# A hybrid trunk layer on one NeuronCore: retention heads moved ahead of the stick-breaking heads of their round

## The chip, the cores and the metric

The kernel runs on one core of a Trainium2 chip. The metric is device time in microseconds (us). The kernel before took a median of 1002.31 us in 3 runs (1002.0 to 1005.52). "About no change" below means within 0.5%.

## What is computed

One layer over 544 rows of 1024 channels (512 rows of a new stream, 32 of a running one). Cut to what matters here:

```python
h = rmsnorm(x, norm_mix_w)
rq, rk, rv, rg, sq, sk, sv, ga, gb = split(h @ w_in)          # nine times 1024 columns
rq, rk = rotary(rq), rotary(rk) / 16                          # 4 retention heads, 256 wide
sq, sk = rmsnorm(sq, q_norm_w), rmsnorm(sk, k_norm_w)         # 8 stick-breaking heads, 128 wide
o_ret = chunkwise_retention(rq, rk, rv)                       # also the new state of each head
z = sq @ sk.T / sqrt(128);  u = log_sigmoid(-z) below the diagonal
o_sb = exp(log_sigmoid(z) + reversed_exclusive_cumsum(u)) @ sv
mix = sigmoid(ga) * rmsnorm(o_ret) * silu(rg) + sigmoid(gb) * o_sb
x = x + mix @ w_out
y = x + square(relu(rmsnorm(x) @ w_up)) @ w_down
```

## The kernel before, in words

Rows lie along the free axis (544 columns, in two halves of 272); channels lie on the 128 partitions. Every float32 product is made of three TensorE products of rounded parts (hi by hi, lo by hi, hi by lo). One **gemm** (function `gemm`) makes 128 output channels: 2 halves x 8 k-tiles x 3 = 48 matmuls of 128x272. Its weight tile comes by DMA on SP's queue (`load_w`), ACT casts it to `whi`, DVE subtracts to `wlo`. There are two buffers of each, so the cast for the gemm after next can't begin before a gemm has ended, and has to be done, `wlo` too, when the one in between ends. Each half goes to one of three PSUM banks (`mm`), which its reader on ACT or DVE gives back.

The order: first seven gemms on rows that are not yet normed (`X`, the input times the norm's weight; their readers multiply by the inverse root mean square `u` afterwards), while DVE and ACT make the normed rows `H`. Then four **rounds**. Round c has two stick-breaking heads (2c, 2c+1) with key, query and value gemms each, then retention head c with two gemms each for key, query and value (in round 0 some of them are among the seven on `X`). Then the **merge**: for each of 8 tiles a gemm for `rg`, one for `ga`, one for `gb`, whose readers on ACT are Sigmoids. Then the output projection and the MLP.

What a head does after its gemms is a **chain**, a Python generator that `Flow` cuts into pieces and puts between the matmuls of later gemms. `Flow` keeps a planned clock of PE, ACT and DVE, counts of free buffers, and runs a chain's next piece when its plan says that the inputs are ready (`poll`, after each k-tile). PE's order is this written order; ACT's and DVE's orders come from a scheduler. The chains named below:

- `sb_chain` (stick-breaking head): scores z into three of five `at` banks; ACT Abs, Exp, Ln; DVE adds max(z, 0) and splits into `sh`, `sl`; PE sums along the keys with the triangular `tri_r` and `neg1_r`; ACT Exp; DVE splits; PE multiplies by the values.
- `qk_chain` (QK norm): sums of squares by `ones_r`, then `rstd` on ACT (Ln, Exp, Square) and DVE.
- `sample_chain` (the 32 rows of the running stream, four heads at once): Abs, Exp, Ln, a scan, Exp, transposes, values.
- `retention_chain`, `ret_sample_chain` (which makes `so` by ACT and DVE and transposes it on PE) and `state_chain` (which transposes decayed keys, casts them to `kt`, and multiplies `rvs` by `kt`).

After the merge's second tile `flow.drain()` runs what is left of the chains. In the kernel before, that is retention head 3.

Of the kernel before, what the change touches and what calls it, by code (L numbers as in the profile page):

```python
# [16 lines left out]
D = 1024  # L17
# [17 lines left out]
IDLE = {0: 5, 1: 3}  # L35

MLP_W = 80
OUT_ORDER = (0, 4, 1, 5, 2, 6, 3, 7)


# [191 lines left out]
def trunk(ctx: ExitStack, tc: tile.TileContext, a: dict, g32):  # L232
# [11 lines left out]
    def tmp():  # L244
        return tp.tile([P, NT], F32, tag="tmp", name="tmp")
# [60 lines left out]
    def gemm(x, read, **parts):  # L306

        flow.wait(**parts)
        w = loaded.pop(0)
        load_w()
        for h in range(2):
            flow.wait(mm=1)
            ps = acc_bank()
            for k in range(KD):
                if x is H:
                    flow.pe = max(flow.pe, flow.done[("h", k)])
                products(ps, w, x, k, h)  # L320
                flow.poll()
            read(h, slice(h * HT, (h + 1) * HT), ps)
            flow.give(mm=1)
# [118 lines left out]
    def sb_value_tiles():  # L442

        hi = qkp.tile([P, 4, P], F32R, tag="vt_hi", name="vt_hi", bufs=2)
        lo = qkp.tile([P, 4, P], F32R, tag="vt_lo", name="vt_lo", bufs=2)
        return hi, lo, qkp.tile([P, P], F32, tag="vt_3", name="vt_3", bufs=2)
# [20 lines left out]
    def rope_tiles(tag):  # L467
        return [qkp.tile([P, NT], F32, tag=f"{tag}{d}", name=f"{tag}{d}") for d in range(2)]

    def rope(x, y, phase, c, n):  # L470


        def first(h, s, p):
            V.tensor_tensor(y[0][:, s], p, phase[0][:, s], op=ALU.mult)
            V.tensor_tensor(y[1][:, s], p, phase[1][:, s], op=ALU.mult)

        def second(h, s, p):
            t1, t2 = t.get()
            V.tensor_tensor(t1[:, s], p, phase[1][:, s], op=ALU.mult)
            V.tensor_tensor(t2[:, s], p, phase[0][:, s], op=ALU.mult)  # L480

        gemm(x, first)
        t = Tmps(2)
        gemm(x, second)
        flow.start(rope_chain(y, *t.get(), c, n))
# [44 lines left out]
    with tc.tile_pool(name="xin", bufs=1, side="right") as xp:  # L530
        xs = []
        x_hi = xp.tile([P, KD, NT], F32R, tag="x_hi", name="x_hi")
        x_lo = xp.tile([P, KD, NT], F32R, tag="x_lo", name="x_lo")
        for k in range(KD):
            t = xp.tile([P, NT], F32, tag=f"x{k}", name=f"x{k}")
            nc.sync.dma_start(out=t, in_=a["x"][k])
            xs.append(t)
            w = wv[:, 0, k : k + 1]
            if k == 0:
                split_scaled(t, w, x_hi[:, k, :], x_lo[:, k, :])  # L540
            else:
                S.activation(x_hi[:, k, :], t, AF.Copy, scale=w)
                V.scalar_tensor_tensor(
                    x_lo[:, k, :], t, w, x_hi[:, k, :].bitcast(F32), op0=ALU.mult, op1=ALU.subtract
                )
            if k in (0, 3):
                load_w()
        load_w(xp)
        nc.vector.tensor_scalar(nw[:, 0, :], wv[:, 0, :], -1.0 / (2 * D), None, op0=ALU.mult)
        nc.vector.tensor_scalar(nw[:, 2, :], wv[:, 2, :], -1.0 / 512, None, op0=ALU.mult)  # L550
        nc.vector.tensor_scalar(nw[:, 3, 0:1], wv[:, 3, 0:1], -(128.0 ** -0.5) / 256, None, op0=ALU.mult)
        nc.vector.tensor_scalar(nw[:, 3, 1:2], wv[:, 3, 1:2], -1.0 / 256, None, op0=ALU.mult)
        nc.sync.dma_start(out=cst, in_=a["cst"])
        X = (x_hi, x_lo)
        u = []

        def first_norm():
            acc = tmp()
            for k in range(KD):
                add_square(acc, xs[k], k == 0)  # L560
            flow.t = 16500.0
            parts = sum_parts(acc)
            yield need(at=2)
            sums = partition_sums(parts)
            flow.t += 2250
            with tc.high_priority():
                u.append(rstd(sums, D))
            flow.give(at=2)
            flow.finish("u")
            scaled(pa, ra, u[0])  # L570
            scaled(pb, rb, u[0])
            flow.give(at=1, mm=3)
            flow.finish("ab")
            flow.start(value_chain(ra, vt0, 0, vs[:, 0, :], ("v", 0), a["o_v"][0]))
            flow.start(value_chain(rb, rv0, 0, rvs0, ("rv0", 0)))
            yield need()
            for k in range(KD):
                t = tmp()
                V.scalar_tensor_tensor(t, xs[k], nw[:, 0, k : k + 1], u[0], op0=ALU.mult, op1=ALU.mult)
                split(t, h_hi[:, k, :], h_lo[:, k, :])  # L580
                flow.finish("h", k)
                if k % 2:
                    yield need()
            flow.give(tmp=6)

        flow.wait(vt=2, rv=1, tmp=9, mm=3, at=1)
        vt0, vt1 = sb_value_tiles(), sb_value_tiles()
        rv0, rvs0 = ret_value_tiles()
        ra, rb, rc = tmp(), tmp(), tmp()
        pa, pb = (acc_bank(), acc_bank()), (acc_bank(), bank()[:, :HT])  # L590
        wa, wb = loaded.pop(0), loaded.pop(0)
        flow.start(first_norm())
        flow.pe = 6500.0
        for k in range(KD + 2):
            for ps, w, kk in ((pa, wa, k), (pb, wb, k - 2)):
                if 0 <= kk < KD:
                    for h in range(2):
                        products(ps[h], w, X, kk, h)
            for i in range(IDLE.get(k, 0)):
                nc.tensor.matmul(idle[:, :P], ones_r, ones_r, start=True, stop=True)  # L600
            flow.poll()
        flow.wait(at=2)
        pc = (bank()[:, :HT], bank()[:, :HT])
        w = loaded.pop(0)
        for k in range(KD):
            for h in range(2):
                products(pc[h], w, X, k, h)
            flow.poll()
            if k == 5:
                load_w()  # L610
        flow.until("ab")
        scaled(pc, rc, u[0])
        flow.give(at=2)
        flow.start(value_chain(rc, rv0, P, rvs0, ("rv1", 0)))
        flow.wait(tmp=1)
        rd = tmp()
        gemm(X, lambda h, c, p: V.scalar_tensor_tensor(
            rd[:, c], p, -1.0 / (2 * D), u[0][:, c], op0=ALU.mult, op1=ALU.mult
        ))
        flow.start(value_chain(rd, vt1, 0, vs[:, 1, :], ("v", 1), a["o_v"][1]))  # L620
        flow.wait(rk=1, tmp=2)
        rk0 = rope_tiles("rk")
        turned = [tmp(), tmp()]
        for t, c0 in zip(turned, (C_COS, C_SIN)):
            V.scalar_tensor_tensor(t, u[0], -1.0 / (2 * D), cst[:, c0 : c0 + NT], op0=ALU.mult, op1=ALU.mult)
        rope(X, rk0, turned, 0, 0)
        flow.give(tmp=2)
        query_key(0, 1, X, u[0])
        flow.until("h", KD - 1)

    bigp = at.enter_context(tc.tile_pool(name="bigp", bufs=1))
# [340 lines left out]
        leave(c)  # L972

    phase = (cst[:, C_COS:C_SIN], cst[:, C_SIN:C_TRI])
    for c in range(NH):
        for h in (2 * c, 2 * c + 1):
            for w_col in (1, 0):
                if (h, w_col) != (0, 1):
                    query_key(h, w_col)
            if c == 0:  # L980
                vt = (vt0, vt1)[h]
            else:
                flow.wait(vt=1)
                vt = sb_value_tiles()
                values(H, vt, 0, vs[:, h % 4, :], ("v", h), a["o_v"][h])
            flow.start(sb_chain(h, vt))
        if c % 2:
            flow.start(sample_chain(c // 2))
        x = []
        for n, tag in enumerate(("rk", "rq")):  # L990
            if c == 0 and n == 0:
                x.append(rk0)
                continue
            flow.wait(**{tag: 1})
            x.append(rope_tiles(tag))
            rope(H, x[n], phase, c, n)
        if c == 0:
            rv, rvs = rv0, rvs0
        else:
            flow.wait(rv=1)  # L1000
            rv, rvs = ret_value_tiles()
            for ei in range(2):
                values(H, rv, ei * P, rvs, (f"rv{ei}", c))
        sc = bigp.tile([P, 2, 256], F32, tag="sc", name="sc")
        nc.gpsimd.dma_start(out=sc, in_=a["state"][c].rearrange("(d p) e -> p d e", p=P))
        flow.start(retention_chain(c, rv))
        flow.start(ret_sample_chain(c, x[0], x[1], rvs, sc))
        flow.start(state_chain(c, x[0], rv, rvs, sc))


    mp = ctx.enter_context(ExitStack())
# [411 lines left out]
```

## Time and profile before

| | us |
|---|---|
| median of 3 runs | 1002.31 |
| the profiled execution | 1002.26 |
| its span | 1000.5 |
| PE busy | 986.7 |
| DVE busy | 668.0 |
| ACT busy | 522.7 |
| matmuls of 128x272 in a steady stream, from start to start | 0.125 |

PE's busy time is made of matmuls that overlap: each shows 0.29 us and they start each 0.125 us. A gap is therefore seen best from start to start; the number in brackets behind a row of the timeline counts from the modelled end of the matmul before. Times in the views are us from the span's start. The seven gemms on `X` end at 54.7 us, the four rounds at about 421 us, the merge begins there.

### The profile page before, as it was taken

The numbers are of one execution on the slowest core, as the hardware profiler recorded it, in microseconds if no ns is written. First come the engines' busy times: TensorE is split into PE (matmuls) and PEld (weight loads), VectorE is DVE, ScalarE is ACT, GpSimd is POOL, SyncE is SP. The second block draws the span as 40 slices with busy tenths as digits, with TensorE's granted clock in tenths as the row PEclk, the third lists the DMA queues.
The fourth block names the chain that finished last, engine by engine and source line by source line (L and its number), as shares of the span: only waits on it lengthen the run. The fifth ranks groups of instructions, "written<-read, shape, count | busy, mean of one in ns | idle before, by whom it ended". The sixth has DMA issues, their size and how long they took to land.

```text
span 1000.5 us, 18622 instructions
## 1 busy us (share of the span) xinstructions
PE 986.7 (99%) x7726; PEld 969.3 (97%) x7726; DVE 668.0 (67%) x1124; ACT 522.7 (52%) x963; POOL 47.2 (5%) x80
## 2 busy tenths in 40 slices
PE   9999999999999999999999999999999999999998
PEld 9999888999999999889999999999999999999998
DVE  7968768866677576756434447974676666676782
ACT  6466756537654675564333335775464445444440
POOL 0000003001000011000000011000000000000000
PEclk9999999999999999999999999999999999999999
DMA  7232224122322135114322245232223332343312
GB/s 253 87 128 75 86 75 149 64 85 96 108 64 85 64 125 164 45 51 165 97 87 85 85 142 185 85 127 85 85 93 101 103 106 87 104 129 96 119 43 90
DMA packets 30932, 102.71 MB, mean 103 GB/s; under 512 B 4096, under 2 KB 6144, under 8 KB 30848
## 3 DMA queue, kind: packets, MB, share of 16 engines
q1 hardware_dynamic: 24768, 80.88, 25.0%
q0 software_dynamic: 6080, 20.65, 6.2%
q8 instruction: 60, 0.98, 0.4%
q14 instruction: 24, 0.20, 0.1%
HBM read 90.51 MB, written 11.01 MB: 101 GB/s over the span
## 4 chain that ended last, share of the span: by engine, by line
PE 95%; ACT 2%; DVE 2%; issue 0%; ACTq 0%; DVEq 0%
PE mm L225 70%; PE at L225 25%; ACT tmp L225 1%; PE at L384 0%; DVE sl L225 0%; ACT e L225 0%; ACT whi L225 0%; ACT L225 0%; DVE tmp L225 0%; ACT kt L225 0%; DVE sh L225 0%; DVE e L225 0%; PE at L600 0%; DVE so L225 0%; ACT st L225 0%
## 5 line engine op out<-in xcount | busy, mean ns | idle before, releaser
L225 PE MATMUL mm<-h_hi,whi 128*128 128x272 f32 x1040 | 304.5, 293 | 0.0
L225 PE MATMUL mm<-h_hi,wlo 128*128 128x272 f32 x1040 | 301.1, 290 | 0.9 <-DVE wlo L225 0.9
L225 PE MATMUL mm<-h_lo,whi 128*128 128x272 f32 x1040 | 300.3, 289 | 0.0
L225 DVE TENSOR_TENSOR wlo<-raw,whi 128x1024 fp32r<-128x1024 f32 (+1 forms) x146 | 167.6, 1150 | 125.8 <-ACT whi L225 125.0
L225 ACT CAST whi<-raw 128x1024 fp32r<-128x1024 f32 (+1 forms) x146 | 144.8, 992 | 179.3 <-PE mm L225 162.1
L225 PEld LDWEIGHTS mm<-h_hi,whi 128*128 128x128 f32 x1040 | 196.7, 189 | 1.9 <-issue 1.3
L225 PEld LDWEIGHTS mm<-h_hi,wlo 128*128 128x128 f32 x1040 | 196.3, 189 | 1.1 <-DVE wlo L225 1.1
L225 PEld LDWEIGHTS mm<-h_lo,whi 128*128 128x128 f32 x1040 | 196.9, 189 | 0.1
L225 PE MATMUL mm<-u_hi,whi 128*128 128x272 f32 x512 | 147.9, 289 | 0.0
L225 PE MATMUL mm<-u_lo,whi 128*128 128x272 f32 x512 | 147.8, 289 | 0.0
L225 PE MATMUL mm<-u_hi,wlo 128*128 128x272 f32 x512 | 147.7, 288 | 0.0
L225 PEld LDWEIGHTS mm<-u_hi,whi 128*128 128x128 f32 x512 | 96.6, 189 | 0.4 <-DVE y L225 0.2
L225 PEld LDWEIGHTS mm<-u_lo,whi 128*128 128x128 f32 x512 | 96.5, 188 | 0.0
L225 PEld LDWEIGHTS mm<-u_hi,wlo 128*128 128x128 f32 x512 | 96.3, 188 | 0.0
L225 PE MATMUL at<-f_hi,wlo 128*128 128x272 f32 x320 | 92.7, 290 | 0.0
L225 PE MATMUL at<-f_lo,whi 128*128 128x272 f32 x320 | 92.2, 288 | 0.0
L225 PE MATMUL at<-f_hi,whi 128*128 128x272 f32 x320 | 92.1, 288 | 0.0
L225 ACT ACTIVATE tmp<-tmp 128x272 f32<-128x272 f32 (+2 forms) x148 | 75.4, 553 | 29.6 <-DVE tmp L225 29.1
L225 DVE TENSOR_TENSOR y<-mm,y 128x272 f32<-128x272 f32 x112 | 48.6, 436 | 29.3 <-PE mm L225 29.3
L225 PEld LDWEIGHTS at<-f_hi,whi 128*128 128x128 f32 x320 | 60.5, 189 | 0.0
L225 PEld LDWEIGHTS at<-f_lo,whi 128*128 128x128 f32 x320 | 60.4, 189 | 0.0
L225 PEld LDWEIGHTS at<-f_hi,wlo 128*128 128x128 f32 x320 | 60.3, 188 | 0.0
(234 smaller groups left out, 1795.0 us busy)
## 6 DMA issues: line engine op xcount, KB each, us to landing
raw<-in_w SPq DMA_DIRECT2D x142, 512.0 KB, 3.5
x<-in_x SPq DMA_DIRECT2D x8, 272.0 KB, 5.2
o_v<-tmp POOLq DMA_DIRECT2D x8, 272.0 KB, 2.4
o_k<-tmp POOLq DMA_DIRECT2D x8, 272.0 KB, 2.5
x<-in_x POOLq DMA_DIRECT2D x8, 272.0 KB, 3.6
o_y<-x POOLq DMA_DIRECT2D x8, 272.0 KB, 2.4
tmp<-o_y POOLq DMA_DIRECT2D x8, 272.0 KB, 3.8
o_y<-y SPq DMA_DIRECT2D x16, 136.0 KB, 1.7
```

The costliest lines, as they stand in the source:

```text
L225: f(out, *args, **kw)
```

## The change

The list `HEADS` now gives the order of the heads: R0 S0 S1 R1 S2 S3 R2 S4 S5 R3 S6 S7 (R is a retention head, S a stick-breaking one). So the retention head comes first in each round, and the last chains are those of stick-breaking heads 6 and 7. The seven gemms on `X` were sv0, rv0 (two), sv1, rk0 (two), sk0; they are now sv0, rv0 (two), rk0 (two), rq0 (two). The values of head 1 and the key of head 0 are made from `H`. The order of the weight tiles in memory follows.

```diff
+HEADS = "R0 S0 S1 R1 S2 S3 R2 S4 S5 R3 S6 S7".split()
...
-        flow.wait(vt=2, rv=1, tmp=9, mm=3, at=1)
-        vt0, vt1 = sb_value_tiles(), sb_value_tiles()
+        flow.wait(vt=1, rv=1, tmp=9, mm=3, at=1)
+        vt0 = sb_value_tiles()
...
-        flow.wait(tmp=1)
-        rd = tmp()
-        gemm(X, lambda h, c, p: V.scalar_tensor_tensor(
-            rd[:, c], p, -1.0 / (2 * D), u[0][:, c], op0=ALU.mult, op1=ALU.mult
-        ))
-        flow.start(value_chain(rd, vt1, 0, vs[:, 1, :], ("v", 1), a["o_v"][1]))
...
         rope(X, rk0, turned, 0, 0)
+        flow.wait(rq=1)
+        rq0 = rope_tiles("rq")
+        rope(X, rq0, turned, 0, 1)
         flow.give(tmp=2)
-        query_key(0, 1, X, u[0])
...
-    for c in range(NH):
-        for h in (2 * c, 2 * c + 1):
-            for w_col in (1, 0):
-                if (h, w_col) != (0, 1):
-                    query_key(h, w_col)
...
+    def stick_breaking(h):
+        for w_col in (1, 0):
+            query_key(h, w_col)
+        if h == 0:
+            vt = vt0
+        else:
+            flow.wait(vt=1)
+            vt = sb_value_tiles()
+            values(H, vt, 0, vs[:, h % 4, :], ("v", h), a["o_v"][h])
+        flow.start(sb_chain(h, vt))
+        if h % 4 == 3:
+            flow.start(sample_chain(h // 4))
+
+    def retention(c):
         if c == 0:
-            rv, rvs = rv0, rvs0
+            k, q, rv, rvs = rk0, rq0, rv0, rvs0
         else:
+            flow.wait(rk=1)
+            k = rope_tiles("rk")
+            rope(H, k, phase, c, 0)
+            flow.wait(rq=1)
+            q = rope_tiles("rq")
+            rope(H, q, phase, c, 1)
...
+    for kind, n in HEADS:
+        (stick_breaking if kind == "S" else retention)(int(n))
```

How it moves instructions. **ACT, at the merge's beginning.** `tmp<-mm` is a Sigmoid on a gemm's half, `e<-at` the Abs or the Exp of a stick-breaking head, `e<-e` its Exp or Ln, `whi<-raw` the cast of a weight tile, `kt` the decayed keys. Before:

```order
L225 ACTIVATE tmp<-mm 128x272
L225 CAST kt_5472<-at 128x512
L225 ACT_TABLE_LOAD
L225 ACTIVATE tmp<-at,epsb 128x512
L225 ACT_TABLE_LOAD
L225 ACTIVATE tmp<-tmp 128x512 x2
L225 COPY so_p<-at 128x512
L225 ACT_TABLE_LOAD
L225 ACTIVATE tmp<-mm 128x272
L225 CAST kt_5529<-at 32x256
```

Now, from the scores of head 7 on, in two pieces that follow each other (the second has head 7's casts `sh`, the Exp and Ln of the sample rows, `tmp<-tmp`, and head 7's last Exps):

```order
L227 ACTIVATE e<-at 128x512 x2
L227 ACTIVATE e<-at 128x256
L227 ACT_TABLE_LOAD
L227 ACTIVATE e<-e 128x1280
L227 ACT_TABLE_LOAD
L227 ACTIVATE tmp<-mm 128x272
L227 ACT_TABLE_LOAD
L227 ACTIVATE e<-e 128x1280
L227 CAST whi<-raw 128x1024
L227 ACT_TABLE_LOAD
L227 ACTIVATE tmp<-mm 128x272 x2
L227 CAST whi<-raw 128x1024
```

```order
L227 ACT_TABLE_LOAD
L227 ACTIVATE tmp<-tmp 128x544
L227 CAST sh<-e 128x128 x3
L227 ACT_TABLE_LOAD
L227 ACTIVATE tmp<-tmp 128x544
L227 ACT_TABLE_LOAD
L227 ACTIVATE e<-at 128x512
L227 ACT_TABLE_LOAD
L227 ACTIVATE tmp<-mm 128x272
L227 ACT_TABLE_LOAD
L227 ACTIVATE tmp<-tmp 128x544
L227 ACTIVATE e<-at 128x512
```

What moved: where four table loads stood in the whole merge before, sixteen stand now, one at each change between a Sigmoid and a chain's Exp or Ln, and one between Exp and Ln (the program has 19 loads in all, 7 before).

**ACT, in the sample rows of retention head 0** (`so` and `st` are theirs; `tmp<-at,epsb` and `tmp<-tmp` are Ln and Exp or Square of a QK norm). Before:

```order
L225 CAST qk_hi_1726<-tmp 128x512
L225 ACTIVATE so,st<-at 32x256
L225 ACTIVATE st<-st,epsb 32x1
L225 ACTIVATE st<-st 32x1 x2
L225 COPY tmp<-mm 128x272
```

Now:

```order
L227 ACTIVATE so,st<-at 32x256
L227 ACTIVATE tmp<-at,epsb 128x272
L227 ACTIVATE st<-st,epsb 32x1
L227 ACTIVATE tmp<-tmp 128x272
L227 ACTIVATE st<-st 32x1
L227 ACTIVATE tmp<-at,epsb 128x272
L227 ACTIVATE st<-st 32x1
L227 ACTIVATE tmp<-tmp 128x272 x3
```

What moved: the norm of head 0's key stands between the steps of `so`, which had ACT to themselves before.

## Rows read from the trace of the kernel before

**Rows 1.** The page: busy time, and the chain that ended last, by engine.

```profile
PE 986.7 (99%) x7726; PEld 969.3 (97%) x7726; DVE 668.0 (67%) x1124; ACT 522.7 (52%) x963; POOL 47.2 (5%) x80
PE 95%; ACT 2%; DVE 2%; issue 0%; ACTq 0%; DVEq 0%
```

**Rows 2.** Busy time by stretch (us; PE, PEld, DVE, ACT, POOL; granted clock; DMA share; GB/s).

```profile
26.00:54.00 28.00, 28.00 (x227) 27.95 (x227) 27.85 (x52) 13.43 (x28) 1.23 (x2) 1.00 0.24 78
85.00:165.00 80.00, 74.12 (x543) 69.67 (x542) 59.97 (x113) 52.76 (x119) 6.90 (x12) 1.00 0.27 88
```

**Rows 3.** PE's waits from 85 to 165 us: total, times, longest; three of eight.

```profile
PE at L225 <- DVE so L225: 1.3, 1, 1.3
PE at L225 <- DVE sl L225: 1.0, 1, 1.0
PE mm L225 <- DVE wlo L225: 0.9, 1, 0.9
```

**Rows 4.** Timeline of PE at the last chain's end (start, busy, row, [idle before <- releaser]).

```profile
449.01 0.29 PE L225 MATMUL mm<-h_hi,wlo 128*128 128x272 f32 x1
451.33 0.50 PE L225 MATMUL at<-rvs,kt 96*128 96x256 f32 x2 [2.03 <-ACT kt L225]
```

**Rows 5.** Busy time by stretch around that wait, columns as in rows 2.

```profile
448.84:452.26 3.42, 1.39 (x11) 1.17 (x10) 3.30 (x6) 2.80 (x6) 0.16 (x1) 1.00 0.22 77
452.26:455.67 3.41, 3.41 (x17) 3.41 (x16) 1.76 (x3) 0.00 (x0) 0.72 (x1) 0.50 0.79 265
455.67:459.08 3.41, 3.41 (x29) 3.41 (x28) 1.22 (x1) 1.47 (x3) 0.00 (x0) 1.00 0.74 275
```

**Rows 6.** Timeline of ACT before that wait.

```profile
446.23 1.30 ACT L225 ACTIVATE tmp<-tmp 128x512 f32<-128x512 f32 x2
...
448.02 1.28 ACT L225 ACT_TABLE_LOAD   x1
449.31 0.40 ACT L225 ACTIVATE tmp<-mm 128x272 f32<-128x272 f32 x1
449.60 0.35 ACT L225 CAST kt<-at 32x256 fp32r<-32x256 f32 x1
```

**Rows 7.** The way to so in retention head 0: timelines of ACT and DVE.

```profile
133.12 0.37 ACT L225 ACTIVATE so<-at 32x256 f32<-32x256 f32 x1
136.07 0.47 DVE L225 TENSOR_SCALAR so<-at,st 32x256 f32<-32x256 f32 x1
```

**Rows 8.** Timelines at the end of the gemms on X; the page's landing times on POOL's queue.

```profile
54.69 0.28 PE L225 MATMUL mm<-h_hi,whi 128*128 128x272 f32 x1
55.45 0.72 POOL L1005 DMA_DIRECT2D sc<-in_state  x1 [17.34 <-DVE neg_r L646]
x<-in_x POOLq DMA_DIRECT2D x8, 272.0 KB, 3.6
```

**Rows 9.** Timeline of ACT in sb_chain of head 0, and pieces of ACT at 406 us.

```profile
82.02 0.87 ACT L225 ACTIVATE e<-at 128x512 f32<-128x512 f32 x2 [0.16 <-PE at L225]
83.15 1.28 ACT L225 ACTIVATE e<-e 128x1280 f32<-128x1280 f32 x1
84.31 0.43 ACT L225 ACTIVATE tmp<-tmp 128x272 f32<-128x272 f32 x1
406.44 1.35 ACT L225 ACTIVATE tmp<-tmp 128x544 f32<-128x544 f32 x2
408.25 0.50 ACT L225 CAST sh<-e 128x128 fp32r<-128x128 f32 x2 [0.27 <-DVE e L225]
```

**Rows 10.** Timeline of DVE: the same head's e, a wlo, and the head's second split.

```profile
85.94 1.62 DVE L225 SCALAR_TENSOR_TENSOR e<-at,e 128x512 f32<-128x512 f32 x3 [1.90 <-ACT e L225]
89.13 1.22 DVE L225 TENSOR_TENSOR wlo<-raw,whi 128x1024 fp32r<-128x1024 f32 x1
105.86 0.83 DVE L225 CAST sh<-e 128x1280 fp32r<-128x1280 f32 x1
106.79 1.49 DVE L225 TENSOR_TENSOR sl<-e,sh 128x1280 fp32r<-128x1280 f32 x1
```

More of the change, by code (lines that the diff above doesn't have):

```diff
@@ L974, in trunk @@
     phase = (cst[:, C_COS:C_SIN], cst[:, C_SIN:C_TRI])
-    for c in range(NH):
-        for h in (2 * c, 2 * c + 1):
-            for w_col in (1, 0):
-                if (h, w_col) != (0, 1):
-                    query_key(h, w_col)
[L980 to L996, printed above, removed]
+    def stick_breaking(h):
[11 more added lines that the diff above has]
+    def retention(c):
         if c == 0:
-            rv, rvs = rv0, rvs0
+            k, q, rv, rvs = rk0, rq0, rv0, rvs0
         else:
+            flow.wait(rk=1)
[4 more added lines that the diff above has]
+            rope(H, q, phase, c, 1)
             flow.wait(rv=1)
@@ L1006, in trunk @@
         flow.start(retention_chain(c, rv))
-        flow.start(ret_sample_chain(c, x[0], x[1], rvs, sc))
-        flow.start(state_chain(c, x[0], rv, rvs, sc))
+        flow.start(ret_sample_chain(c, k, q, rvs, sc))
+        flow.start(state_chain(c, k, rv, rvs, sc))
+    for kind, n in HEADS:
+        (stick_breaking if kind == "S" else retention)(int(n))
     mp = ctx.enter_context(ExitStack())
@@ L1351 @@
     ws = []
-    ws += [sv[0], rv[0], rv[1], sv[1], rk[0], rk[1]]
-    for c in range(NH):
-        for h in (2 * c, 2 * c + 1):
-            ws += [sk[h], sq[h], sv[h]][: 2 if c == 0 else 3]
-        for p in (rk, rq, rv) if c else (rq,):
-            ws += [p[2 * c], p[2 * c + 1]]
+    ws += [sv[0], rv[0], rv[1], rk[0], rk[1], rq[0], rq[1]]
+    for kind, n in HEADS:
+        n = int(n)
+        if kind == "S":
+            ws += [sk[n], sq[n], sv[n]] if n else [sk[n], sq[n]]
+        elif n:
+            ws += [p[2 * n + i] for p in (rk, rq, rv) for i in range(2)]
     for t in range(KD):
```

## The prediction

> **What bounds the kernel now.** First the page's busy times and the chain that ended last [rows 1]: PE is busy 986.7 of 1000.5 us and holds 95% of the chain. Both programs give PE the same 7598 matmuls, so a new order can only win or lose PE's waits and the clock. Then the windows and PE's waits. In 85 to 165 us, where the first round's chains meet, PE is idle for 80.00 - 74.12 = 5.9 us [rows 2], in eight waits of which three stand in [rows 3]. Idle time counts from the modelled end of a matmul, 0.29 us after its start, where the stream would have gone on after 0.125; each wait costs some 0.15 us more, so about 7.0 us in all. The second place is the end of the last chain: PE's product of `rvs` and `kt` starts 451.33 - 449.01 = 2.3 us after the matmul before it [rows 4], which is 2.2 lost. Behind it the granted clock fell: after a stretch with 11 matmuls came one of 3.41 us at 0.50 (the 1.2 GHz level) with 17 records, where the next at full clock has 29 [rows 5]. 12 x 0.125 = 1.5 us lost. So the tail costs 2.2 + 1.5 = 3.7 us. What PE waited for there is ACT: its queue had table loads of 1.28 us each, one Sigmoid and then the cast `kt` [rows 6]. The rest of the rounds shows under 1.5 us of waits; they are built alike before and after, and I leave them at no change.
>
> **The change, part by part: the start.** Ahead of the first round, rq0 takes the place of sv1 and sk0 on `X`. DVE gets 8 reads of 272 columns, two sums and two splits in a stretch where it has no idle time (27.85 of 28.00 us) [rows 2]. It did 52 instructions there; from 27.0 us on it now has 51 of the same kinds (27.3 us by the same mean) up to the last normed rows, and waits for PE about 1 us: 55.5 us; PE begins with `H` at 54.7 [rows 8] and reaches the last k-tile 21 matmuls later, at 57.3. Covered, with 1.8 us to spare. POOL's loads for retention head 0 (`sc`, `dm`, `dec`) went out at 55.45 behind DVE's cast `neg_r` [rows 8]; that cast now stands behind the sums of rq0, at about 57.7. `dm` follows `sc` by 0.7 and lands 3.6 later, at 62.0; it is read when PE has done 57 gemm matmuls and six score products, at 63.3. Covered too, by 1.3 us. The next `dm` and `dec` now stand ahead of `o_k` of head 0 on POOL, but its key is finished later still. SP has the same weight tiles in another order.
>
> The old waits go: the second split of head 0 has 7 us of PE work before its values now, and the value copies of head 3 no longer stand between a chain and its banks. Two new ones come, both seen in the order of ACT.
> - `so` of retention head 0. From the last product PE to ACT takes 0.3. ACT now does 0.37 + 0.2 for `so` and, with the key's norm between, three pieces of 0.35 and three of 0.2 to 0.3: 2.3. DVE adds four short ones and a product of 544: 1.6. Together 4.2 us. PE has four sums and 12 matmuls, 2.0 us. Wait: **2.2** us. Before it took 136.07 - 133.12 us to the last step [rows 7], beside 18 matmuls. Bounds: 1.2 (that wait again) to 3.
> - `kt` of the sample rows. It is cast behind the norm of head 1's key: 0.25 to reach ACT, two Ln of 0.37, an Exp of 0.35, the cast 0.36, 1.7 us, while PE has three matmuls, 0.4. Wait: **1.3** us (0 to 2).
> - Two more are small differences of long sums (the sums of squares of sk1, the `wlo` of rk1's second tile), 0.45 each: **0.9** us (0 to 2).
>
> The start then keeps 4.5 of its 7.0 us: **-2.5** (from -5.8 to 0).
>
> **The tail.** The last chains are now those of heads 6 and 7 and of the sample rows; their Exp and Ln alternate with the merge's Sigmoids. Sixteen table loads stand there instead of four: 12 x 1.28 = 15.4 us more on ACT. What of it reaches PE I take from four places, with pieces from start to start: 1.29 a load, 0.3 a Sigmoid [rows 6], 0.3 the last Abs, 1.16 for 1280 columns, 0.6 for 544, 0.2 a cast `sh` [rows 9].
> - **Weights of ga1.** After head 7's last score: 0.25, Abs 0.3, load, Exp 1.16, load, Sigmoid 0.3, load, Ln 1.16 is 7.0; then DVE's three pieces of `e` 1.55 and `wlo` 1.2 [rows 10]: 9.7. The cast's buffer is free long before. PE has 6 + 48 + 2 matmuls, 7.0 us, until it needs `wlo`. Wait: **2.7**.
> - **Head 7's sums over keys.** After the sample scores: 0.25, Abs 0.35, load 1.29, Exp 0.6, two casts 0.4 is 2.9; PE has 6 matmuls and two products, 1.2. Wait: **1.6** (the table load and the Exp alone make it).
> - **The sample weights' transposes.** From there ACT does the third cast, load, Ln 0.6, load, Exp 0.5, load, Sigmoid 0.3, load, Exp 0.6: 7.4; PE has sums of 1.55 and 30 matmuls, 5.3. Wait: **1.9** (with the cast shared, 2.1 at most).
> - **Head 7's values.** Two Exps 0.8, then `sh` 0.83 and `sl` 1.49 [rows 10]: 3.0; PE has transposes, 9 matmuls and one product, 1.9. Wait: **1.1**.
>
> Sum 7.3 us. Bounds: 2.2 (no worse than now) to 11, if each place is 1 us later. The first hole, 2.7 us with two matmuls in it, is longer than the one behind which the clock fell before [rows 4, 5], so I count one fall, 1.5 us; bounds none to three. Tail 8.8 against 3.7: **+5.1** (from -1.5 to +11.8).
>
> On the loads a rule has to be weighed. In the trace the Sigmoid starts 449.31 - 448.02 = 1.29 us after the load's start, and the Exp before it follows a load as closely [rows 6]. The Trainium skill, "ScalarE: Activation LUTs", section "What ACT_TABLE_LOAD costs", gives about 1283 ns for the load and about 1380 ns for a drain with every switch, 2.66 us together. The load agrees with the row, the drain isn't seen in it. By the page twelve loads would add 31.9 us to ACT instead of 15.4.
>
> **Sum:** -2.5 + 5.1 = +2.6 us on the profiled execution's 1002.26: 1004.9. The median of the runs, 1002.31, is the same within 0.1 us.
>
> **The rivals.**
> - **The loads are covered.** If PE finds the chains done at the four places, the tail loses its 3.7 us and the start 2.5: 1002.3 - 6.2 = 996.1; with half of the waits left, about 999.5. For it: ACT is busy for 52% only [rows 1]. Against it: at the last chain a single queue of three loads already made 2.3 us [rows 4, 6]. It needs PE's 7.0 us at ga1 to outlast 9.7. Chance 0.10.
> - **The tail is ACT's, and the clock falls again** (slower). One fall stretches PE's next pieces, the sample scores come later, and all that ACT does behind them too. It decides as soon as the second hole also holds over 2 us: then two more falls, 3.0 us, and 1 us more at each of two places, 1002.3 + 2.6 + 5 = 1009.9. For it: the holes stand within 20 us. Against it: a fall that PE spends waiting anyway costs nothing. Chance 0.27.
> - **The start wins nothing.** DVE falls behind on rq0, PE waits at the first k-tiles of `H`, and the eight waits come back in other places: 1002.3 + 5.1 = 1007.4. For it: no idle time on DVE [rows 2]. Chance 0.12.
> - **The drain counts too.** With each switch some 1.4 us longer, the three, one and four loads at the first three places make 4.1, 1.4 and 5.5 us more, 1016. The rows show no such gap [rows 6]. Chance 0.01. This is the price of the skill's page named above.
> - The forecast: 0.50.
>
> **How the numbers follow.** A measurement of this kernel tells 0.5%, 5.0 us, from no change. Faster by more (under 997.3): most of the half-covered case stays inside, so 0.06. Slower by more (over 1007.3): most of the second rival (0.22), half of the third (0.06), the drain (0.01) and the forecast's upper bounds (0.05): 0.34. Within: 0.60. The range reaches from the half-covered case, 999.5, to 1010.5, just past the second rival.
>
> **What would show it.** Right: ACT with 19 table loads of 1.28 us; from 85 to 165 us PE idle for under 5 us, with a wait for `so` of about 2 us near 71 us; after the scores of head 7 a wait for `wlo` of over 2 us and three more of 1 to 2 us; the granted clock at 0.50 at least once there; the MLP unchanged. Wrong: no wait over 1 us in the merge (the loads are covered), or waits before 60 us (DVE is late). Were the sum of waits in the merge right and the time still near 1000, the start would have won more than I give it.

## The result and the profile after

The changed kernel took a median of 1008.81 us in 4 runs (1008.53 to 1009.9) where the kernel before took 1002.45 beside it: a ratio of 1.0059, 95% interval 1.0038 to 1.008. Run again later on another occasion (experiment e11) it took 1008.38 us, a ratio of 1.0044 (1.0031 to 1.0058). So it is slower, by about the 0.5% that the prediction set as its bound; 0.5% lies inside both intervals. The profiled execution took 1008.78 us, its span 1007.0.

The page of the changed kernel, busy times and the chain that ended last (against [rows 1]):

```profile
PE 989.6 (98%) x7726; PEld 969.5 (96%) x7726; DVE 665.6 (66%) x1120; ACT 539.4 (54%) x979; POOL 45.8 (5%) x80
PE 93%; ACT 4%; DVE 3%; issue 0%; DVEq 0%
```

ACT has 16 instructions and 16.7 us more, PE the same 7726 matmuls, DVE four instructions and 2.4 us less; ACT and DVE now hold 7% of the chain instead of 4%. The groups of ACT's table loads, first of the kernel before, then of the changed one (instructions, busy us, mean ns):

```profile
L225 ACT ACT_TABLE_LOAD x6 | 7.7, 1283 | 0.1
```

```profile
L227 ACT ACT_TABLE_LOAD x18 | 23.1, 1283 | 0.3
```

One more in each has a line of its own. Seven loads became 19; 12 x 1.283 = 15.4 us is nearly all of ACT's growth. Sixteen of them stand in the merge.

Where PE waits now, in the changed kernel from 55 to 180 us (total, times, longest; against [rows 3]), and then from 421 to 501 us, the merge up to its fourth tile:

```profile
PE at L227 <- DVE so L227: 2.0, 2, 1.9
PE at L227 <- ACT kt L227: 1.0, 1, 1.0
PE at L227 <- DVE tmp_r L227: 0.3, 1, 0.3
```

```profile
PE at L227 <- ACT tmp L227: 1.9, 1, 1.9
PE mm L227 <- ACT whi L227: 1.7, 1, 1.7
PE at L227 <- ACT sh L227: 1.5, 1, 1.5
PE mm L227 <- DVE wlo L227: 1.3, 1, 1.3
PE at L227 <- DVE sl L227: 1.1, 1, 1.1
```

To see the whole span on one scale, take each matmul's start less the start of the matmul before it, and subtract the usual distance of the same two kinds of product (the lower quartile over the program). What is left is time that PE lost, to waits, to the clock and to many gaps too small to name:

| PE's lost us | gemms on `X` | start, to 180 us | rounds, to the merge | merge, 3 tiles | rest | sum |
|---|---|---|---|---|---|---|
| before | 6.6 | 11.3 | 10.6 | 6.1 | 7.3 | 41.9 |
| changed | 7.6 | 7.9 | 11.7 | 13.8 | 7.4 | 48.4 |
| difference | +1.0 | -3.4 | +1.1 | +7.7 | +0.1 | +6.5 |

The sum is the difference of the two spans, 1007.0 - 1000.5. The start did win, and the merge lost twice as much. The +1.0 on `X` goes with the clock: full clock was granted from 14.14 us on in this execution, from 11.94 us in the one before, and the first gemm on `H` begins at 55.23 instead of 54.69 us. It belongs to the execution and not to the order: the profile of e12, with the same seven gemms on `X`, has full clock from 11.19 us and loses 6.3 us there.

**The first hole of the merge**, ACT's timeline of the changed kernel from head 7's last scores on:

```profile
446.19 0.87 ACT L227 ACTIVATE e<-at 128x512 f32<-128x512 f32 x2 [0.16 <-PE at L227]
447.08 1.28 ACT L227 ACT_TABLE_LOAD   x1
448.38 1.27 ACT L227 ACTIVATE e<-e 128x1280 f32<-128x1280 f32 x1
449.67 1.28 ACT L227 ACT_TABLE_LOAD   x1
450.96 0.40 ACT L227 ACTIVATE tmp<-mm 128x272 f32<-128x272 f32 x1
451.38 1.28 ACT L227 ACT_TABLE_LOAD   x1
452.67 1.27 ACT L227 ACTIVATE e<-e 128x1280 f32<-128x1280 f32 x1
453.85 1.03 ACT L227 CAST whi<-raw 128x1024 fp32r<-128x1024 f32 x1
```

Between Exp and Ln of one head stand a load, one Sigmoid of a gemm and another load; the cast `whi` for the gemm of ga1 comes last in that queue. DVE follows:

```profile
453.98 1.62 DVE L227 SCALAR_TENSOR_TENSOR e<-at,e 128x512 f32<-128x512 f32 x3 [1.10 <-ACT e L227]
455.51 1.22 DVE L227 TENSOR_TENSOR wlo<-raw,whi 128x1024 fp32r<-128x1024 f32 x1
```

and PE waits for `whi` first, for `wlo` then, and at three more places (PE's timeline; the last number is the idle time before the row):

```profile
454.93 0.39 PE L227 MATMUL mm<-h_hi,whi 128*128 128x272 f32 x1 [1.65 <-ACT whi L227]
...
456.78 0.39 PE L227 MATMUL mm<-h_hi,wlo 128*128 128x272 f32 x1 [1.34 <-DVE wlo L227]
...
464.56 0.44 PE L227 MATMUL at<-sh,neg_r 128*128 128x384 f32 x1 [1.48 <-ACT sh L227]
...
472.30 0.76 PE L227 MATMUL at<-cst,tmp 128*128 128x128 f32 x5 [1.94 <-ACT tmp L227]
...
475.52 0.50 PE L227 MATMUL at<-sl,vt_hi 128*128 128x512 f32 x1 [1.08 <-DVE sl L227]
```

These are the four places of the prediction, in its order; the first hole is split in two waits. On ACT's way to the third place stand two table loads between Exp and Ln with no Sigmoid between:

```profile
464.72 1.28 ACT L227 ACT_TABLE_LOAD   x1
466.01 0.66 ACT L227 ACTIVATE tmp<-tmp 128x544 f32<-128x544 f32 x1
466.69 1.28 ACT L227 ACT_TABLE_LOAD   x1
467.99 0.60 ACT L227 ACTIVATE e<-at 128x512 f32<-128x512 f32 x1
```

The first row's load follows the sample rows' Exp; then come their Ln, a load, and head 7's Exp. With one more at 435.68 us, behind the Ln of a norm, three of the sixteen loads stand so, where the section on the change has one. The clock by stretch (columns as in [rows 2]):

```profile
454.00:457.88 3.88, 1.61 (x10) 1.40 (x11) 3.88 (x7) 3.78 (x5) 0.00 (x0) 1.00 0.03 4
457.88:461.29 3.41, 3.41 (x35) 2.55 (x33) 3.34 (x5) 0.13 (x1) 0.00 (x0) 0.50 0.69 222
```

One fall to 0.50 for 3.41 us, behind the stretch in which PE was busy for 1.61 of 3.88 us, as in the kernel before [rows 5].

### The profile page after: what moved, and what is told of

Its sections match the earlier page's. It is cut to its first block, busy times and chain, and to the rows that moved or that the text cites. A ratio compares the mean times of both kernels' runs of the same rounds, so it can differ in the third digit from the quotient of the medians.

```text
span 1007.0 us, 18627 instructions
## 1 busy us (share of the span) xinstructions
PE 989.6 (98%) x7726; PEld 969.5 (96%) x7726; DVE 665.6 (66%) x1120; ACT 539.4 (54%) x979; POOL 45.8 (5%) x80
## 4 chain that ended last, share of the span: by engine, by line
PE 93%; ACT 4%; DVE 3%; issue 0%; DVEq 0%
PE mm L227 68%; PE at L227 25%; ACT tmp L227 1%; ACT L227 1%; ACT e L227 1%; DVE sl L227 1%; DVE tmp L227 1%; PE at L386 0%; ACT whi L227 0%; DVE sh L227 0%; DVE e L227 0%; DVE wlo L227 0%; DVE so L227 0%; PE at L602 0%; DVE pt L227 0%
```

## The experiments

The theory at the outset: all of the loss comes from the merge, where table loads hold up ACT's queue; the start wins some 3 us, by the new order of the heads. The rivals: two stick-breaking heads' chains are too long for the merge, loads or not; or the start wins nothing that lasts. Ratios are to runs of the kernel before on the same chip; its median there was 1004.2 to 1004.8 us.

### e1 and e2: one end of the new order at a time

```diff
-HEADS = "R0 S0 S1 R1 S2 S3 R2 S4 S5 R3 S6 S7".split()
+HEADS = "R0 S0 S1 R1 S2 S3 R2 S4 S5 S6 S7 R3".split()
```

> The new start with the tail of the kernel before: retention head 3 is last again (order R0 S0 S1 R1 S2 S3 R2 S4 S5 S6 S7 R3), 7 table loads. My theory (the start wins about 3 us, the rounds give about 1 us back, all of the loss is in the merge): 1002.4 - 3.1 + 1.1 = 1000.4 us, between 999.3 and 1001. Rival (the start wins nothing that lasts, waits only move): 1002.4 us or more.

Measured: 1003.36 us, ratio 0.9996 (0.9987 to 1.0004). By the time the rival came, and waits did move; but where to, neither theory said. By the method of the table the start lost 7.6 us and the merge 3.9, both as I expected or better, but the rounds lost 15.5 instead of 11.7. PE's waits from 355 to 370 us say where:

```profile
PE at L227 <- DVE tmp_r L227: 1.2, 1, 1.2
PE at L227 <- DVE sl L227: 0.7, 1, 0.7
```

The longest two of three stand here; the kernel before has none in these 15 us. The edit put four stick-breaking heads in a row (S4 to S7), and their chains and norms meet without a retention head's six gemms between. What it won at both ends it lost in the rounds.

The other hybrid is the kernel before, with its seven gemms on `X` and its start, and only retention head 3 moved ahead of heads 6 and 7. Against the changed kernel:

```diff
-HEADS = "R0 S0 S1 R1 S2 S3 R2 S4 S5 R3 S6 S7".split()
+HEADS = "S0 S1 R0 S2 S3 R1 S4 S5 R2 R3 S6 S7".split()
...
```

(The rest of the edit brings back the old seven gemms on `X`.)

> The start of the kernel before with the new tail: stick-breaking heads 6 and 7 last (order S0 S1 R0 S2 S3 R1 S4 S5 R2 R3 S6 S7), 19 table loads. My theory: the merge costs what it costs in the changed kernel, about 6 us more than before, so 1008.4 us, and as the start wins nothing here it may reach 1010. Rival (the loss comes from the order of the rounds or the start, and the tail by itself is mostly covered): under 1005 us.

Measured: 1021.85 us, ratio 1.0168 (1.0154 to 1.0182), far above both. The merge lost 12.2 us, 6.1 more than before, which is what the theory said. But two retention heads now stand side by side, and PE waits there; the longest waits from 300 to 350 us, and the clock behind the first hole:

```profile
PE at L227 <- DVE so L227: 3.5, 1, 3.5
PE at L227 <- ACT kt L227: 1.9, 1, 1.9
```

```profile
325.73:329.14 3.41, 3.27 (x12) 2.92 (x13) 1.18 (x4) 0.59 (x1) 0.00 (x0) 0.50 0.02 7
```

So neither hybrid isolates an end: a head moved to keep one end makes a new crowd in the middle. They confirm only the merges' own sums.

### e3 and e4: the same order without the table loads

```diff
-            S.activation(sg[:, c], p, AF.Sigmoid)
+            S.activation(sg[:, c], p, AF.Exp if t < 2 else AF.Sigmoid)
...
```

(the same for `sa` and `sb`.)

> The changed kernel, with Exp in the place of Sigmoid on the gates of the merge's first two tiles, so that those two tiles of the mix are another function; this takes away the switches between Sigmoid and the chains' Exp and Ln (table loads 19 to 4), and nothing else on any engine. My theory (the table loads hold ACT's queue, and PE waits behind it): the waits at the four places shrink from about 9.4 us to under 3, the clock no longer falls, 1008.8 - 6.5 - 1.5 = 1000.8 us, within 1.5. Rival (two stick-breaking heads' chains are simply longer than the cover that the merge has, loads or not): 1007 us or more.

Measured: 998.72 us, ratio 0.9945 (0.9933 to 0.9958), 10 us under the changed kernel and 2.1 under my own 1000.8. The order of PE's instructions is the same as in the changed kernel. ACT's page line lost 15 instructions and 19.0 us, which are the loads; PE's waits from 410 to 505 us are down to one of 0.4:

```profile
PE 988.3 (99%) x7726; PEld 970.0 (97%) x7726; DVE 665.6 (67%) x1120; ACT 520.4 (52%) x964; POOL 45.9 (5%) x80
```

```profile
PE at L227 <- ACT sh L227: 0.4, 1, 0.4
```

ACT's timeline of the same place shows the queue closed up: from Exp to the cast's start it takes 2.6 us, where it took 5.5.

```profile
448.56 1.27 ACT L227 ACTIVATE e<-e 128x1280 f32<-128x1280 f32 x1
449.73 0.38 ACT L227 ACTIVATE tmp<-mm 128x272 f32<-128x272 f32 x1
450.01 1.26 ACT L227 ACTIVATE e<-e 128x1280 f32<-128x1280 f32 x1
451.17 1.04 ACT L227 CAST whi<-raw 128x1024 fp32r<-128x1024 f32 x1
```

By the table's method the merge lost 3.9 us instead of 13.8. As PE runs the same matmuls in the same order, the two merges can also be compared start by start: of the 9.9 us, 7.8 are what the five waits grew by, and 1.5 stand at the matmuls from 457.8 to 461.6 us, where the clock had fallen in the changed kernel. The rival that the chains are too long by themselves falls.

```diff
+    def gate(out, p, t):
+        if t >= 2:
+            S.activation(out, p, AF.Sigmoid)
+            return
+        S.activation(out, p, AF.Exp, scale=-1.0)
+        S.activation(out, out, AF.Ln, bias=1.0)
+        S.activation(out, out, AF.Exp, scale=-1.0)
...
```

(`gate` then takes the place of the three Sigmoids.)

> The changed kernel, with the Sigmoid of the merge's first two tiles made of Exp, Ln and Exp: 4 table loads instead of 19, but two more pieces of ACT of some 0.35 us for each of 12 halves, 8.4 us, beside 15 x 1.28 = 19.2 us of loads saved. My theory (what counts is the load between two pieces of a chain, not ACT's total): 1001 to 1003 us. Rival (ACT's total busy time in the stretch decides): about 11 of 19 us are saved, so a little over half of the loss goes, about 1004 to 1005 us.

Measured: 1000.27 us, ratio 0.9961 (0.9948 to 0.9974), a little under my own 1001 to 1003. ACT is busy 530.0 us, 9.4 less than in the changed kernel and 9.6 more than in e3; yet 8.5 of the 10 us are won. What counts is the load inside a chain, not ACT's sum. This is the remedy that the Trainium skill names in "ScalarE: Activation LUTs", section "Table sets: the hidden batching unit" (group the calls by table set), done here by writing one function with those of the other set; the run agrees.

### e7: the loads in the plan

`Flow`'s plan gives every ACT piece 0.92 ns a column and 70 ns, and knows no table load. Here it does; the Sigmoids stay.

```diff
...
+                kind = {AF.Sigmoid: "sigmoid", AF.Exp: "exp", AF.Ln: "exp"}.get(func)
+                if kind and kind != self.table:
+                    extra, self.table = 1290 * (self.table is not None), kind
+            self.flow.ran(self.lane, self.length(name, out, args) + extra)
```

> The changed kernel with its Sigmoids kept, and 1290 ns added in the plan of ACT wherever Sigmoid and Exp or Ln follow each other; the order of PE then puts the chains' pieces later between the merge's matmuls, and 17 table loads are left of 19. My theory (PE waits because the written order counts no table load, so its pieces stand too early): the waits of the merge fall from 9.4 to about 4 us and the clock does not fall, 1008.8 - 5.4 - 1.5 = 1002 us, within 1.5. Rival (ACT with its loads is late by itself, and pieces put later only reach the end of the second tile without cover): 1006 us or more.

Measured: 1004.76 us, ratio 1.0003 (0.9994 to 1.0012), between what the two theories said. PE's waits from 410 to 505 us:

```profile
PE at L228 <- ACT sh L228: 1.9, 1, 1.9
PE at L228 <- DVE sl L228: 1.1, 2, 0.8
PE mm L228 <- DVE wlo L228: 0.2, 1, 0.2
```

The waits for `whi` and for the sample rows' transposes are gone, those at head 7's sums are longer, and the clock fell for twice as long there (6.83 us). The merge lost 9.9 us instead of 13.8. So about 4 of the 7.7 us went with a plan that counts the loads (and has two fewer of them); the rest stayed. Whether another plan would hide it too with the loads in was not tried.

### e6, e8 and e12: the start's two waits, and everything together

```diff
         S.activation(st[:, 2:3], st[:, 1:2], AF.Square)
...
+        if c == 0:
+            flow.t += 2200
...
+        if c == 0:
+            flow.t += 1800
```

(in `ret_sample_chain` behind `so`, and in `state_chain` ahead of the product of `rvs` and `kt`.)

> The changed kernel, with the plan of round 0 told that so is done 2.2 us later and the piece before the product of rvs and kt 1.8 us later, so that both stand some gemm matmuls further back in the order of PE. My theory (the two waits at 72 and 97 us, 1.7 and 1.2 us, are work of ACT and DVE that PE reached too early): both waits go, 1008.8 - 2.9 = 1006 us, within 1. Rival (ACT and DVE are behind as such there, and PE waits at the next piece instead): 1008.8 us.

Measured: 1004.06 us, ratio 0.9997 (0.9987 to 1.0006), 4.3 to 4.7 us under the changed kernel, more than expected. Both waits are gone; from 55 to 180 us this is all that is left:

```profile
PE at L227 <- DVE so L227: 0.4, 1, 0.4
```

The start lost 4.5 us instead of 7.9 and the rounds 10.5 instead of 11.7: with pieces of round 0 put later, small waits of the later rounds go too, which I had not expected; how was not traced.

> The three-step gates of the merge's first two tiles together with the later pieces of round 0. If the two do not touch each other: 1000.3 - 2.9 = 997.4 us, within 1. If the waits of round 0 only move: 1000.3 us.

Measured: 996.46 us, ratio 0.9918 (0.9904 to 0.9932). The two edits add up (3.8 us under e4).

e12 is e8 with one edit more, in `sb_chain`:

```diff
         later_parts(e, parts)
+        if h == 7:
+            flow.t += 1800
         yield need()
```

> The changed kernel with the three-step gates and the later pieces of round 0, and head 7's sums over keys planned 1.8 us later, four gemm matmul triples further back. What is left in the merge without that are two waits at those sums, 0.9 us for sl and 1.3 us for sh. My theory (again only the place in the written order): both go, 996.5 - 2.2 = 994.3 us. Rival (the chains behind it, head 7's values and the sample rows, now meet nearer to the end of the second tile and wait there): 996.5 us or more.

Measured: 992.67 us, ratio 0.9889 (0.9874 to 0.9904), better than both kernels and than expected. Of PE's waits in the merge the view from 410 to 505 us shows one, and the clock stays full from 11.2 to 990.8 us:

```profile
PE at L227 <- ACT sh L227: 0.5, 1, 0.5
```

### e9: the new order without its new first gemms

```diff
-    ws += [sv[0], rv[0], rv[1], rk[0], rk[1], rq[0], rq[1]]
+    ws += [sv[0], rv[0], rv[1], sv[1], rk[0], rk[1], sk[0]]
...
-        rope(X, rq0, turned, 0, 1)
+        query_key(0, 1, X, u[0])
...
+            q = rope_tiles("rq")
+            rope(H, q, phase, c, 1)
```

> The new order of heads with the seven first gemms of the kernel before (sv0, rv0, sv1, rk0, sk0 on rows not yet normed; the two of rq0 are made from normed rows). It undoes the one part of the change and keeps the other. My theory (the 3 us won at the start come from the order of the heads): 1008.8 us, within 1.5. Rival (they come from rq0 on rows not yet normed): the waits return, 1011.8 us or more.

Measured: 1025.26 us, ratio 1.0211 (1.0195 to 1.0227). My theory falls, by more than the rival said. PE's longest waits from 55 to 180 us, and the clock (windows):

```profile
PE at L227 <- ACT tmp_r L227: 4.5, 1, 4.5
PE at L227 <- DVE so L227: 2.7, 1, 2.7
PE at L227 <- DVE sl L227: 1.7, 1, 1.7
PE at L227 <- DVE tmp_r L227: 1.2, 1, 1.2
```

```profile
87.00:90.60 3.60, 1.45 (x10) 1.20 (x8) 3.21 (x8) 3.60 (x9) 0.55 (x1) 1.00 0.00 0
90.60:104.25 13.65, 7.41 (x21) 5.71 (x22) 11.02 (x23) 7.90 (x17) 0.54 (x1) 0.50 0.22 63
```

With sv1 and sk0 already made on `X`, heads 0 and 1 bring three and not five gemms behind retention head 0's chains, and all chains of the round meet over them. The start lost 20.8 us instead of 7.9. The two parts of the change need each other: the new order makes the start better than the old one only with the new first gemms. Whether that is the query that is ready early, or the cover of the two gemms more that heads 0 and 1 then bring, this run can't tell, as it changes both.

### e10 and e11: is the order worth anything, and the changed kernel again

e10 is the kernel before with the `gate` of e4 and no other edit; e11 is the changed kernel, unedited.

> The kernel before with the three-step gates of the merge's first two tiles, 4 table loads instead of 7. It tells whether the new order is worth anything once the loads are gone. My theory: the wait for kt (2.2 us, behind loads) and the clock's fall behind it (1.5 us) go, so 3.7 us off the kernel before, a ratio of 0.9963 to it and about the same time as the changed kernel with these gates. Rival (retention head 3's chain is late without the loads too): under 1.5 us off, a ratio over 0.9985.

Measured: 1001.0 us, ratio 0.9968 (0.9955 to 0.9981), as the theory said: the kernel before had this loss too, in small. Its eight waits of the start stay (1.4, 1.3, 1.0, 0.9 and four of 0.2 to 0.4 us from 55 to 180 us). Against e4 (0.9961) the new order is worth nothing that can be told; with the pieces of e12 it reaches 0.9889. Whether the old order, with its pieces put later in the same way, would reach as far was not tried.

> The changed kernel again, as it is, beside the same runs of the kernel before as the others. What was measured first was a ratio of 1.0059 (1.0038 to 1.008). If the loss is no matter of the chip or of the few runs then: a ratio between 1.0038 and 1.008 again, so some 6 us over the kernel before. If it was: under 1.0038.

Measured: 1008.38 us (1008.1 to 1008.7), ratio 1.0044 (1.0031 to 1.0058): the loss is there again, at the lower edge. The clock goes with that: these five runs have a mean granted clock of 0.998, but of the 13 runs of the kernel before only the three of 1001.87 to 1001.98 us have it; the other ten show 0.997 and took 1003.06 to 1005.59 us. At the same mean clock the changed kernel is 6.4 us longer, as in the profiles.

## Why the prediction was right, and where it was off

The time, 1008.8, is inside the range of 999.5 to 1010.5 and 3.9 us above the 1004.9 forecast. By the table's columns these 3.9 are +1.0 on `X` (the clock of that execution, in no part of the forecast), -0.9, +1.1, +2.6 and +0.1. The likeliest case was "about no change"; what came lies on the bound between that and "slower by over 0.5%", with 0.59% the first time and 0.44% in e11. Some of the sums are off by 0.1 or 0.2 us (27.0 + 27.3 + 1 is 55.3 and not 55.5; 2.9 - 1.2 is 1.7 and not 1.6), and both pages count 7726 matmuls where the prediction has 7598; nothing hangs on either.

- **The start, -2.5 forecast, -3.4 found.** The mechanism holds: the old eight waits went, and the two new ones came where the order showed them (the first at 72.42 us). From start to start `so` cost 1.7 us (2.2 forecast), `kt` 1.2 (1.3), the two small ones 0.5 and 0.3 (0.9 together). No wait came before 60 us, so DVE did keep up with rq0, and `dm` was in time. e9 shows that this gain rests on the new first gemms too; the prediction asked only what they cost, and not what they buy.
- **The rounds, "no change" forecast, +1.1 found.** This step failed. The rounds are built alike, but eleven gaps of 0.17 to 0.33 us stand there, 2.7 us together where the kernel before has 1.1 (the first is behind `tmp_r`, at 187.39 us). e6 takes it away (10.5) by moving pieces of round 0 alone, so it belongs to the written order; by what path is open.
- **The tail, +5.1 forecast, +7.7 found.** The four places and their order were right. From start to start they cost 3.3 (2.7 forecast), 1.6 (1.6), 2.1 (1.9) and 1.3 us (1.1): 8.3 against 7.3; the sums were mis-sized, not the mechanism. At ga1 ACT took 453.85 - 446.19 = 7.7 us from its last two Abs to the cast behind Ln, where I had counted 6.8 with one Abs; DVE's part, 2.75 us, was as counted. PE waited there for `whi` before it waited for `wlo`, which alone I had named. One fall of the clock came, as forecast, and cost the 1.5 us forecast (by the comparison with e3; the sample scores, which ran inside it, took 1.7 instead of 1.1 us). That makes 8.3 + 1.5 - 3.7 = 6.1 of the 7.7; the other 1.6 us are spread over gaps of up to 0.2 us, to which the prediction gave nothing. Some 0.9 of them is in e3 too, so it goes with the order and not with the loads. e3 shows the cause of the rest: without the loads the same order loses 3.9 us there.
- **The rivals.** "The loads are covered" falls with the merge's waits. "The tail is ACT's and the clock falls again" is near by its time (1009.9) but not by its mechanism: in the profile the clock fell once, and the second hole held 1.6 us, under the 2 us from which that case was to decide. One of the nine runs of the changed kernel may have been that case, 1009.9 us at a mean clock of 0.995 where the other eight show 0.998; it has no profile. "The start wins nothing" falls with the start's column. The drain: the load starts 0.02 us behind the Abs and the Exp 448.38 - 447.08 = 1.30 us after the load. Set beside e3, two loads make the queue from Exp to cast 5.47 - 2.61 = 2.86 us longer, 1.43 each, as pieces with no load between them overlap by 0.1 us. The drain that the Trainium skill adds ("ScalarE: Activation LUTs", "What ACT_TABLE_LOAD costs") isn't seen in this trace either.
- **Of the signs** all but one came as worded: 19 loads, under 5 us idle from 85 to 165 us (1.5), `so` near 72 us, three waits of 1 to 2 us behind the first hole, the clock at 0.50, the MLP unchanged. A wait of over 2 us for `wlo` did not: it was 1.34 us, behind 1.65 us for `whi`.

## What to carry to other kernels

Where pieces of a chain are laid between another stage's matmuls, ask which table set each stage's functions need: a load between two pieces costs at least its 1.28 us on the chain's own path, even on an engine that is half idle. Look for it in the trace between Exp and Ln too. Follow the queue to what stands last in it; here a weight cast behind a chain's Ln held up the gemms themselves. And a plan that orders work ahead of time should count the switches, or its pieces come too early. Where that isn't enough, one function written with those of the other set may be cheaper than the switch: here two more pieces for each half, 9.6 us on ACT for 24 of them, against 15 loads of 1.28 us.

## What the runs showed of the hardware that I had not expected

The same hole doesn't always bring the clock down. Six profiles have the same matmuls up to the wait for `so` and the same wait; in e3 and e4 the clock fell there, in the changed kernel, e1, e7 and e11 it did not. In the changed kernel and in e3 PE does the same up to 72.54 us, and is busy for 1.68 of 3.54 us with the wait for `so`; the granted clock then stays in the one and falls in the other. First the changed kernel, then e3 (windows):

```profile
69.00:72.54 3.54, 1.68 (x15) 1.46 (x13) 3.54 (x8) 3.13 (x12) 0.28 (x1) 1.00 0.30 74
72.54:75.95 3.41, 3.41 (x25) 3.24 (x26) 2.89 (x9) 0.62 (x1) 0.81 (x2) 1.00 0.27 82
```

```profile
69.00:72.54 3.54, 1.68 (x14) 1.46 (x13) 3.54 (x8) 3.20 (x13) 0.20 (x1) 1.00 0.29 74
72.54:75.95 3.41, 3.41 (x15) 3.35 (x16) 2.97 (x9) 0.62 (x1) 0.88 (x2) 0.50 0.29 82
```

That execution of e3 took 1000.41 us, its others 998.6 to 998.8. Runs of the kernel before range from 1001.87 to 1005.87 us; the mean granted clock of each run goes with it. Of the 51 beside the experiments 13 show 0.998 and took 1001.87 to 1003.21 us, the other 38 show 0.996 or 0.997 and took 1003.06 to 1005.87 us. One fall of 3.41 us to 0.50 takes 0.0017 off the mean of 1000 us, so the longer runs had, by estimate, one fall more; where it stood is open, since only one run is profiled. The kernel with almost no holes, e12, spread over 1.0 us only (992.42 to 993.43).
